# The end of a two-layer decoder trunk on one core: residual transposed into the accumulator, a root in PSUM, one eviction per bank, and a new order of the last parts

## The chip, the core and the metric

The kernel runs on one core of a Trainium2 chip. The metric is the device time in microseconds (us) of one execution; lower is better.

## What is computed

A stream of 2048 positions with 1024 features, all in float32, passes through two layers and a last normalisation. Cut to what matters here:

```python
h = rmsnorm(x, norm_a); b, c, xin, g = split(h @ w_in_a, 4)
x1 = x + (b * causal_conv3(c * xin) * silu(g)) @ w_out_a
k, v = split(rmsnorm(x1, norm_kv) @ w_kv, 2)
q, g = split(rmsnorm(x1, norm_b) @ w_in_b, 2)
o = stick_breaking_attention(q, k, v)        # 8 heads of 64, strictly causal
x2 = x1 + (o * silu(g)) @ w_out_b
out = rmsnorm(x2, norm_f)   # y * rsqrt(mean(y*y) + 1e-6) * norm_f
```

The change is mostly about the last two lines, for the last 128 positions. The root, `rsqrt`, is also used by every other normalisation.

## The kernel before

**Layout.** The input and the output are transposed: rows of 128 features lie on the partitions, positions along the free axis. The positions are cut into four chunks `c` of `CH` = 512. A float32 matrix product is made of three products of rounded halves (fp32r, a high and a low part), except for small ones in full float32 such as transposes, which the trace shows as one or two records each.

**Order.** Nearly all of the program is first recorded and then given an order by a planner; every instruction of it is emitted by one line (365), so rows of the profile are told apart by their tiles. Each piece of work belongs to a named part, and the table `PLAN` gives each part two numbers; an instruction's key is interpolated between them, and never lies before that of what it depends on (`places`). `order` then simulates the five engines with the estimated durations of `cost`: of what could start, it takes what could start first, and among equals that with the lower key. Numbers in `PLAN`, estimates in `cost` and dependencies all change which instruction stands before which in each engine's queue. An engine executes its queue in order. In `cost`, `o.turns` marks operations on DVE and POOL with more than one operand in SBUF and none in PSUM; the planner lets them take turns.

**Root.** `rstd` sums a tile of squares over the partitions by products with a column of ones, into a tile `pst_...`, and calls `rsqrt` (line 476). It makes `v` (mean plus epsilon), shifts it, makes a first guess `y` with one integer operation, and runs three steps of three operations on DVE, 12 operations in all:

```python
for _ in range(3):
    nc.vector.tensor_mul(t, y, y)
    nc.vector.scalar_tensor_tensor(out=t, in0=t, scalar=-0.5, in1=v, ...)
    nc.vector.scalar_tensor_tensor(out=y, in0=t, scalar=1.5, in1=y, ...)
```

`bcast` spreads the result over the partitions by four transposes on PE (`prb_...`); `pbs_...` is a copy of it in SBUF for POOL.

**The last layer.** In the names below, `ot` is an attention output, to which POOL adds `v_first` and which it multiplies by the gate `sga`; ACT rounds it to `og`. PE multiplies `og` by `wob` into a bank `pob`; DVE adds it to x1; squares are summed; and the tiles are multiplied by the broadcast root and stored, by POOL for chunks 0 and 1 and by DVE for chunk 2 (`out_kept`, `norm_kept`).

**The end.** `out_last(3)` treats the last chunk in two pieces. The first 384 positions go as above, with three of the eight tiles scaled by POOL (`x<-x,pbs`) and five by DVE (`x<-x,prb_x`). The last 128 positions are exchanged: positions lie on the partitions. While the first piece is computed, each x1 tile's last 128 columns are transposed by PE to `pt`, and ACT copies them to `turned`. Then 12 products with `og` as the stationary operand fill a bank `last` of 512 features, 24 in all for two halves. DVE adds `last` to `turned`; ACT squares it and sums along the row into `sums`; DVE adds the two sums to `total` and runs the root on one column (`v_last`, `t_last`, `yr_last`). DVE scales the identity by the root (`dg`), and PE multiplies blocks of `turned` by `dg`, which transposes back and scales at once, into a bank `back` per half. Each bank is evicted in four blocks of 128x128, ACT and DVE in turn, with the gain of each feature, into one tile `done`; SP's queue stores the first half and ACT's the second.

Behind it, outside of the planner's part, stands a branch with the whole attention done by another method, which runs only if a flag is set; it does not run here.

Of the kernel before, what the change touches and what calls it, by code (L numbers as in the profile page):

```python
# [16 lines left out]
P = 128  # L17
# [167 lines left out]
class Recorder:  # L185
# [30 lines left out]
    def cost(self, o, out, rest):  # L216
# [14 lines left out]
        if kind == PE:  # L231
            if o.name == "transpose":
# [141 lines left out]
def kernel(  # L374
# [967 lines left out]
    def out_last(c):  # L1342
# [14 lines left out]
        for ob in range(KD):  # L1357
# [3 lines left out]
            if ob % 4 == 0:  # L1361
                pt = psum.tile([P, CH], F32, name=f"pt_{c}_{ob}", tag="av", bufs=NAV)
            nc.tensor.transpose(pt[:, (ob % 4) * P:(ob % 4 + 1) * P], x[:, n:CH], ident)
            if ob % 4 == 3:
                nc.scalar.copy(turned[:, ob // 4, :], pt)
# [154 lines left out]
```

## Time and profile before

| | |
|---|---|
| time, median of 3 runs | 1344.25 us (1343.61 to 1344.61) |
| the profiled execution's own time | 1343.01 us |
| its span | 1341.2 us |
| mean granted PE clock | 0.993 |
| ACT busy | 601.9 us (45%) |
| POOL busy | 443.6 us (33%) |
| DMA | 364.99 MB, mean 272 GB/s |

The profile is of one execution. Its engines are PE (matrix products; PEld are PE's weight loads), DVE, ACT and POOL (element-wise work), and SP, which issues transfers; a "q" behind an engine's name stands for its queue of issues. In lists of groups each row gives engine, operation, output and inputs, partitions x elements of both, how often, then the busy time in us and the mean in ns of one, then the engine's idle time just before and what ended it. In lists by time each row starts with the start in us from the beginning of the span and the busy us. Where one row holds several instructions of a kind (x8), its time is that from the first's start to the last's end. A square bracket gives the idle time ahead of a row and who ended it.

### The profile page before, as it was taken

What the parts mean: (1) busy time and instruction counts of PE and PEld (TensorE: products, weight loads), DVE (VectorE), ACT (ScalarE), POOL (GpSimd) and SP (SyncE); (2) the same over time, 40 slices, a digit from 0 to 9 for tenths busy, and PEclk for the clock granted to TensorE, in tenths of its full rate; (3) what the DMA queues carried; (4) which work ended last, traced back from release to release, by engine and by line L of the source; (5) the groups of instructions that cost most, each with busy time, mean ns of one, the idle gap of its engine ahead of it and who ended that gap; (6) DMA issues with size and microseconds to landing.
All of it is one profiled execution on the core that took longest, in us unless ns stands there. A gap on an engine that the chain in (4) does not pass through costs nothing.

```text
span 1341.2 us, 19087 instructions
## 1 busy us (share of the span) xinstructions
PE 1305.6 (97%) x6222; PEld 1082.7 (81%) x6222; DVE 1026.6 (77%) x1626; ACT 601.9 (45%) x1062; POOL 443.6 (33%) x554
## 2 busy tenths in 40 slices
PE   8999999999999999999999999999999999999995
PEld 6888888888888888888788778788778888888884
DVE  7899866689964655656869579887998886898855
ACT  7344534444422332323334344544556554566652
POOL 5252110001000000010032454335357676458971
PEclk9999999999999999999999999999999999999997
DMA  9439879778898799987999876876787677999633
GB/s 327 169 131 325 283 270 326 280 280 292 309 353 287 257 353 334 318 293 244 357 324 325 302 261 209 274 252 230 240 305 233 194 230 244 341 335 310 223 136 128
DMA packets 213276, 364.99 MB, mean 272 GB/s; under 512 B 17028, under 2 KB 98992, under 8 KB 213168
## 3 DMA queue, kind: packets, MB, share of 16 engines
q1 hardware_dynamic: 211920, 362.61, 78.6%
q8 instruction: 51, 0.84, 0.2%
q10 hardware_dynamic: 1120, 1.05, 0.2%
q14 instruction: 57, 0.47, 0.1%
q0 software_dynamic: 128, 0.02, 0.0%
HBM read 217.35 MB, written 146.28 MB: 271 GB/s over the span
## 4 chain that ended last, share of the span: by engine, by line
PE 79%; DVE 12%; POOL 3%; issue 3%; ACT 2%; DMA 1%; SPq 0%; DVEq 0%; POOLq 0%; ACTq 0%
PE fa_C L365 11%; PE fa_B L365 10%; PE fa_o L365 6%; PE fa_kq L365 6%; PE fd_C L365 6%; PE fa_vg L365 5%; PE fd_B L365 5%; PE pob L365 3%; PE fd_vg L365 3%; PE fe_C L365 3%; PE fd_kq L365 3%; PE fd_o L365 3%; PE fe_B L365 3%; PE av L365 2%; PE fe_vg L365 1%
## 5 line engine op out<-in xcount | busy, mean ns | idle before, releaser
L365 POOL COPY halo<-p 128x2 f32<-128x2 f32 x32 | 16.3, 510 | 434.0 <-DVE p L365 434.0
L365 POOL TENSOR_TENSOR acc_x<-acc_x,sq_x 128x512 f32<-128x512 f32 (+1 forms) x53 | 75.8, 1434 | 121.8 <-ACT sq_x L365 121.0
L365 PE MATMUL pob<-og,wob 128*128 128x512 f32 (+1 forms) x384 | 103.6, 397 | 0.5 <-DVE x L365 0.5
L365 PE MATMUL fa_C<-op_t,whl_s_C 128*128 128x512 f32 x336 | 83.3, 389 | 0.0
L365 PE MATMUL fa_B<-op_t,whl_s_B 128*128 128x512 f32 x336 | 82.4, 390 | 0.2 <-ACT f_B L365 0.2
L365 DVE TENSOR_TENSOR_SCAN R<-R,ones 128x192 f32<-128x192 f32 x128 | 79.3, 657 | 2.0 <-POOL R L365 1.8
L365 PEld LDWEIGHTS fa_B<-op_t,whl_s_B 128*128 128x128 f32 x336 | 62.9, 188 | 13.6 <-ACT f_B L365 0.6
L365 PEld LDWEIGHTS fa_C<-op_t,whl_s_C 128*128 128x128 f32 x336 | 63.0, 188 | 13.1
L365 PEld LDWEIGHTS pob<-og,wob 128*128 128x128 f32 x384 | 65.2, 189 | 8.2 <-DVE x L365 0.9
L365 DVE SCALAR_TENSOR_TENSOR cv<-p,cols_of,cv 128x512 f32<-128x512 f32 x64 | 50.3, 787 | 11.0 <-ACT cv L365 10.8
L365 ACT ACTIVATE sq_x<-x 128x512 f32<-128x512 f32 (+1 forms) x56 | 34.4, 617 | 45.7 <-DVE x L365 34.1
L365 ACT CAST wth<-wt 128x512 fp32r<-128x512 f32 x64 | 36.4, 573 | 39.5 <-PE wt L365 19.7
L365 ACT ACTIVATE cv<-p,cols_of 128x512 f32<-128x512 f32 x32 | 23.2, 725 | 67.9 <-DVE p L365 67.9
L365 PE MATMUL wt<-ident,R 128*128 128x128 f32 x248 | 49.0, 274 | 1.5 <-DVE R L365 0.9
L365 POOL TENSOR_SCALAR_AFFINE_SELECT R<-R 128x256 f32<-128x256 f32 x64 | 36.0, 570 | 39.3 <-ACT R L365 39.1
L365 DVE TENSOR_TENSOR wtl<-wt,wth 128x512 fp32r<-128x512 f32 x64 | 42.0, 664 | 7.3 <-ACT wth L365 6.9
L365 PE MATMUL fa_C<-op_b,whl_a_C 128*128 128x512 f32 x168 | 43.1, 390 | 0.0
L365 PE MATMUL fa_B<-op_t,whl_a_B 128*128 128x512 f32 x168 | 43.0, 389 | 0.0
L365 PE MATMUL fe_B<-op_b,whl_a_B 128*128 128x512 f32 x168 | 42.9, 390 | 0.0
L365 PE MATMUL fd_C<-op_t,whl_s_C 128*128 128x512 f32 x168 | 42.3, 390 | 0.2 <-DVE op_t L365 0.2
L365 PE MATMUL fe_C<-op_b,whl_a_C 128*128 128x512 f32 x168 | 42.0, 389 | 0.0
L365 PE MATMUL fd_C<-op_b,whl_s_C 128*128 128x512 f32 x168 | 41.7, 390 | 0.0
(1039 smaller groups left out, 3846.2 us busy)
## 6 DMA issues: line engine op xcount, KB each, us to landing
sw_s_C<-whl_s_C SPq DMA_DIRECT2D x32, 512.0 KB, 3.9
sw_s_B<-whl_s_B SPq DMA_DIRECT2D x32, 512.0 KB, 4.2
q<-q_d SPq DMA_DIRECT2D x32, 512.0 KB, 5.7
sw_a_C<-whl_a_C SPq DMA_DIRECT2D x24, 512.0 KB, 3.3
sw_a_B<-whl_a_B SPq DMA_DIRECT2D x24, 512.0 KB, 3.3
whl_s_C<-sw_s_C SPq DMA_DIRECT2D x24, 512.0 KB, 5.4
whl_s_B<-sw_s_B SPq DMA_DIRECT2D x24, 512.0 KB, 5.3
whl_s_o<-sw_s_o SPq DMA_DIRECT2D x24, 512.0 KB, 5.3
```

The lines of the kernel that those rows point to most:

```text
L365: getattr(o.engine.engine, o.name)(*map(real, o.args), **{k: real(v) for k, v in o.kw.items()})
```

## The change

There are five edits.

- **Residual.** DVE copies the last 128 columns of each x1 tile to `x1_end`. PE transposes these eight blocks straight into the banks `last`, ahead of the products, which accumulate on top. The tile `pt` and the addition on DVE are gone. ACT squares the bank itself and copies it to `turned`, now one tile per half.
- **Root.** `newton` is split from `rsqrt`, for all roots: the first operation of a step is now `t = v * y` and the second multiplies by `-0.5 * y`. For the last root, `v` and `t` are columns of a PSUM tile `room`, so that operations with two tensor operands have one of them in PSUM. The first half's sum is scaled while the second half runs, and one operation scales the second and adds the two.
- **Eviction.** Each bank `back` is evicted by one DVE multiplication of 128x512, with the gains of four feature blocks broadcast along the free axis, into a buffer of its own.
- **Estimates.** `cost` takes transposing products as transposes, and the estimate of a one-column float32 product falls from 0.2 to 0.13.
- **`PLAN`.** The numbers of the last parts are others. A line of the table:

```diff
-    "n2": (1456.2, 1834.4), "o3": (2579.2, 2849.85), "n3": (1413.59, 1415.36), "le": (1301.17, 2112.05),
+    "n2": (2208.71, 2231.02), "o3": (2845.46, 3158.14), "n3": (1326.66, 1619.9), "le": (1768.92, 1896.9),
```

The code of the other edits:

```diff
-            if o.name == "transpose":
+            if o.name == "transpose" or o.kw.get("is_transpose"):
                 o.busy, o.late = 0.1085, 0.36
...
-                o.busy = (0.2 if n == 1 else 0.96 * n / 512) if full else max(0.109, 0.0135 + n / 2400)
+                o.busy = (0.13 if n == 1 else 0.96 * n / 512) if full else max(0.109, 0.0135 + n / 2400)
...
+        return newton(v, t, y)
+
+    def newton(v, t, y):
...
-        for _ in range(3):
-            nc.vector.tensor_mul(t, y, y)
-            nc.vector.scalar_tensor_tensor(out=t, in0=t, scalar=-0.5, in1=v, op0=ALU.mult, op1=ALU.mult)
+        for i in range(3):
+            nc.vector.tensor_mul(t, v, y)
+            nc.vector.scalar_tensor_tensor(out=t, in0=t, scalar=-0.5, in1=y, op0=ALU.mult, op1=ALU.mult)
             nc.vector.scalar_tensor_tensor(out=y, in0=t, scalar=1.5, in1=y, op0=ALU.add, op1=ALU.mult)
...
-            nc.tensor.transpose(pt[:, (ob % 4) * P:(ob % 4 + 1) * P], x[:, n:CH], ident)
-            if ob % 4 == 3:
-                nc.scalar.copy(turned[:, ob // 4, :], pt)
+            nc.vector.tensor_copy(x1_end[:, ob, :], x[:, n:CH])
...
+            for j in range(4):
+                nc.tensor.matmul(ps[:, j * P:(j + 1) * P], x1_end[:, 4 * half + j, :], ident, is_transpose=True, start=j == 0,
+                                 stop=False, skip_group_check=True)
...
-                    nc.tensor.matmul(ps, og_t[c][k][:, m, n:CH], wob[half][k][:, w, :], start=i == 0, stop=i == 11)
+                    nc.tensor.matmul(ps, og_t[c][k][:, m, n:CH], wob[half][k][:, w, :], start=False, stop=i == 11, skip_group_check=True)
...
-            row = turned[:, half, :]
-            nc.vector.tensor_add(row, row, ends[half])
-            nc.scalar.activation(sq, row, AF.Square, accum_out=sums[:, half:half + 1])
-        nc.vector.tensor_add(total[:, 0:1], sums[:, 0:1], sums[:, 1:2])
-        y = rsqrt(total, "last", n=1)
+            nc.scalar.activation(sq, ends[half], AF.Square, accum_out=sums[:, half:half + 1])
+            nc.scalar.copy(turned[half], ends[half])
+            if half == 0:
+                nc.vector.tensor_scalar(out=sums[:, 0:1], in0=sums[:, 0:1], scalar1=1.0 / D, scalar2=EPS, op0=ALU.mult, op1=ALU.add)
+        room = psum.tile([P, CH], F32, name="room", tag="av", bufs=NAV)
+        v, t = room[:, 0:1], room[:, 1:2]
+        nc.vector.tensor_scalar(out=v, in0=sums[:, 1:2], scalar1=1.0 / D, scalar2=sums[:, 0:1], op0=ALU.mult, op1=ALU.add)
+        newton(v, t, y_end)
...
-            for j in range(4):
-                if j % 2:
-                    nc.vector.tensor_scalar(out=done[:, half, blk], in0=ps[:, blk], scalar1=gains["f"][:, ob:ob + 1], ...)
-                else:
-                    nc.scalar.activation(done[:, half, blk], ps[:, blk], AF.Copy, scale=gains["f"][:, ob:ob + 1])
+            done = sb.tile([P, CH], F32, name=f"done_{half}", tag="vv", bufs=2)
+            nc.vector.tensor_mul(done.rearrange("p (j k) -> p j k", j=4), ps.rearrange("p (j k) -> p j k", j=4),
+                                 gains["f"][:, 4 * half:4 * half + 4].unsqueeze(2).to_broadcast([P, 4, P]))
```

The order of the instructions changes in many places. In the rows below a number after a name tells one buffer from another. DVE's queue at the very end, before the change, from the sum of the two halves on; the names with `last` are the root's columns, the five products scale tiles of the last chunk's first piece:

```order
L365 TENSOR_TENSOR total<-sums 128x1
L365 TENSOR_SCALAR v_last<-total 128x1
L365 TENSOR_SCALAR t_last<-v_last 128x1
L365 TENSOR_SCALAR yr_last<-t_last 128x1
L365 TENSOR_TENSOR x_3_0_12940<-x_3_0_12940,prb_x_13237 128x384
L365 TENSOR_TENSOR x_3_1_12965<-x_3_1_12965,prb_x_13237 128x384
L365 TENSOR_TENSOR x_3_2_13001<-x_3_2_13001,prb_x_13237 128x384 x2
L365 TENSOR_TENSOR x_3_3_13029<-x_3_3_13029,prb_x_13237 128x384
L365 TENSOR_TENSOR t_last<-yr_last 128x1
L365 SCALAR_TENSOR_TENSOR t_last<-t_last,v_last 128x1
L365 SCALAR_TENSOR_TENSOR yr_last<-t_last,yr_last 128x1
```

The same place after the change:

```order
L365 TENSOR_SCALAR room<-sums 128x1
L365 TENSOR_SCALAR room<-room 128x1
L365 TENSOR_TENSOR x_3_0_12936<-x_3_0_12936,prb_x_13240 128x384
L365 TENSOR_TENSOR x_3_1_12958<-x_3_1_12958,prb_x_13240 128x384
L365 TENSOR_TENSOR x_3_2_12993<-x_3_2_12993,prb_x_13240 128x384 x2
L365 TENSOR_TENSOR x_3_3_13026<-x_3_3_13026,prb_x_13240 128x384
L365 TENSOR_SCALAR yr_last<-room 128x1
L365 TENSOR_TENSOR room<-room,yr_last 128x1
L365 SCALAR_TENSOR_TENSOR room<-room,yr_last 128x1
L365 SCALAR_TENSOR_TENSOR yr_last<-room,yr_last 128x1
```

Four small operations ahead of the five products have become two; the guess `yr_last` has gone behind them, and no operation of the root has two operands in SBUF.

On POOL some 40 us before the end, with the attention outputs `ot_2` and `ot_3` of the last chunk, the scaling of chunk 1's eight tiles `x_1` and a copy `left` of the check for the flag, before the change:

```order
L365 TENSOR_TENSOR ot_2_12765<-ot_2_12765,v_first 128x512
L365 TENSOR_TENSOR ot_2_12765<-ot_2_12765,sga_2_12051 128x512
L365 TENSOR_TENSOR x_1_0_11936<-x_1_0_11936,pbs_12837 128x512
L365 COPY left<-R_7_1_12749 128x2
L365 TENSOR_TENSOR x_1_0_11936<-x_1_0_11936,pbs_12837 128x512
L365 TENSOR_TENSOR x_1_1_11960<-x_1_1_11960,pbs_12837 128x512 x2
L365 TENSOR_TENSOR x_1_2_12063<-x_1_2_12063,pbs_12837 128x512 x2
L365 TENSOR_TENSOR x_1_3_12442<-x_1_3_12442,pbs_12837 128x512 x2
L365 TENSOR_TENSOR acc_x_12577<-acc_x_12577,sq_x_12833 128x512
L365 TENSOR_TENSOR ot_3_11429<-ot_3_11429,v_first 128x512
```

The same place after the change:

```order
L365 TENSOR_TENSOR ot_2_12312<-ot_2_12312,v_first 128x512
L365 TENSOR_TENSOR x_1_0_11883<-x_1_0_11883,pbs_12834 128x512 x2
L365 TENSOR_TENSOR x_1_1_12013<-x_1_1_12013,pbs_12834 128x512 x2
L365 TENSOR_TENSOR x_1_2_12064<-x_1_2_12064,pbs_12834 128x512 x2
L365 TENSOR_TENSOR x_1_3_12141<-x_1_3_12141,pbs_12834 128x512 x2
L365 TENSOR_TENSOR ot_2_12312<-ot_2_12312,sga_2_11950 128x512
L365 TENSOR_TENSOR ot_3_12757<-ot_3_12757,v_first 128x512
L365 TENSOR_TENSOR ot_3_12757<-ot_3_12757,sga_3_12232 128x512
```

The gate of `ot_2` stood ahead of the eight products of `x_1` and now stands behind them; the sum and the gate of `ot_3` follow without squares between.

On DVE at the beginning of the program, with the first chunk's eight normalised tiles `h_0` to `h_7` and the first root (`v_h`, `t_h`, `yr_h`), - is before and + after:

```order
 L365 SCALAR_TENSOR_TENSOR h_0_557<-xh_0_489,g_a,h_0_557 128x512
+L365 TENSOR_SCALAR v_h_679<-pst_h_663 128x4
+L365 TENSOR_SCALAR t_h_683<-v_h_679 128x4
+L365 TENSOR_SCALAR yr_h_685<-t_h_683 128x4
+L365 TENSOR_TENSOR t_h_683<-v_h_679,yr_h_685 128x4
 L365 SCALAR_TENSOR_TENSOR h_1_572<-xh_1_496,g_a,h_1_572 128x512
-L365 TENSOR_SCALAR v_h_681<-pst_h_663 128x4
-L365 TENSOR_SCALAR t_h_685<-v_h_681 128x4
-L365 TENSOR_SCALAR yr_h_688<-t_h_685 128x4
-L365 TENSOR_TENSOR t_h_685<-yr_h_688 128x4
+L365 SCALAR_TENSOR_TENSOR t_h_683<-t_h_683,yr_h_685 128x4
 L365 SCALAR_TENSOR_TENSOR h_2_605<-xh_2_515,g_a,h_2_605 128x512
```

The first four operations of the root have moved ahead of the product `h_1`; `h_1` has moved behind them.

More of the change, by code (lines that the diff above doesn't have):

```diff
@@ L1354, in out_last @@
         late = []
-        turned = sb.tile([P, 2, CH], F32, name="turned", tag="act", bufs=NA)
-        pt = None
+        turned = [sb.tile([P, CH], F32, name=f"turned_{i}", tag=("wth", "wtl")[i], bufs=NWTS) for i in range(2)]
+        x1_end = sb.tile([P, KD, P], F32, name="x1_end", tag="q2", bufs=2)
         for ob in range(KD):
@@ L1360, in out_last @@
             tag, bufs = (("lin", NLIN), ("z", NZ))[ob % 2]
-            if ob % 4 == 0:
-                pt = psum.tile([P, CH], F32, name=f"pt_{c}_{ob}", tag="av", bufs=NAV)
-            nc.tensor.transpose(pt[:, (ob % 4) * P:(ob % 4 + 1) * P], x[:, n:CH], ident)
-            if ob % 4 == 3:
-                nc.scalar.copy(turned[:, ob // 4, :], pt)
+            nc.vector.tensor_copy(x1_end[:, ob, :], x[:, n:CH])
             ps = psum.tile([P, CH], F32, name=f"pob_{c}_{ob}", tag=tag, bufs=bufs)
@@ L1406, in out_last @@
         for half in range(2):
-            row = turned[:, half, :]
-            nc.vector.tensor_add(row, row, ends[half])
-            sq = sb.tile([P, CH], F32, name=f"sq_last_{half}", tag="q2", bufs=2)
-            nc.scalar.activation(sq, row, AF.Square, accum_out=sums[:, half:half + 1])
-        total = sb.tile([P, 4], F32, name="total", tag="sv")
-        nc.vector.tensor_add(total[:, 0:1], sums[:, 0:1], sums[:, 1:2])
-        y = rsqrt(total, "last", n=1)
+            sq = sb.tile([P, CH], F32, name=f"sq_last_{half}", tag="kt", bufs=2)
+            nc.scalar.activation(sq, ends[half], AF.Square, accum_out=sums[:, half:half + 1])
[4 more added lines that the diff above has]
+        v, t = room[:, 0:1], room[:, 1:2]
+        y_end = sb.tile([P, 4], F32, name="yr_last", tag="sy")[:, 0:1]
+        nc.vector.tensor_scalar(out=v, in0=sums[:, 1:2], scalar1=1.0 / D, scalar2=sums[:, 0:1], op0=ALU.mult, op1=ALU.add)
+        newton(v, t, y_end)
         dg = sb.tile([P, P], F32, name="dg", tag="q2", bufs=2)
-        nc.vector.tensor_scalar(out=dg, in0=ident, scalar1=y, scalar2=None, op0=ALU.mult)
-        done = sb.tile([P, 2, CH], F32, name="done", tag="act", bufs=NA)
+        nc.vector.tensor_scalar(out=dg, in0=ident, scalar1=y_end, scalar2=None, op0=ALU.mult)
         for half in range(2):
@@ L1419, in out_last @@
             for j in range(4):
-                nc.tensor.matmul(ps[:, j * P:(j + 1) * P], turned[:, half, j * P:(j + 1) * P], dg, start=True, stop=True)
-            for j in range(4):
-                ob = 4 * half + j
-                blk = slice(j * P, (j + 1) * P)
-                if j % 2:
-                    nc.vector.tensor_scalar(out=done[:, half, blk], in0=ps[:, blk], scalar1=gains["f"][:, ob:ob + 1], scalar2=None, op0=ALU.mult)
-                else:
-                    nc.scalar.activation(done[:, half, blk], ps[:, blk], AF.Copy, scale=gains["f"][:, ob:ob + 1])
+                nc.tensor.matmul(ps[:, j * P:(j + 1) * P], turned[half][:, j * P:(j + 1) * P], dg, start=True, stop=True)
+            done = sb.tile([P, CH], F32, name=f"done_{half}", tag="vv", bufs=2)
+            nc.vector.tensor_mul(done.rearrange("p (j k) -> p j k", j=4), ps.rearrange("p (j k) -> p j k", j=4),
+                                 gains["f"][:, 4 * half:4 * half + 4].unsqueeze(2).to_broadcast([P, 4, P]))
             (nc.scalar if half else nc.sync).dma_start(
                 out=outT[4 * half * P:4 * (half + 1) * P, S - CH * c - P:S - CH * c].rearrange("(k p) n -> p k n", p=P),
-                in_=done[:, half, :].rearrange("p (k n) -> p k n", k=4))
+                in_=done.rearrange("p (j k) -> p j k", j=4))
     def part(name, f, *args):
```

26 rows, old and new, of the table PLAN are left out of this document.

## The prediction, made before the changed kernel was run

> **What bounds the kernel now.** I read the page first, then who waits on TensorE, then the chain of work that ended last, and at its end the instructions in order of time.
>
> ```profile
> span 1341.2 us, 19087 instructions
> PE 1305.6 (97%) x6222; PEld 1082.7 (81%) x6222; DVE 1026.6 (77%) x1626; ACT 601.9 (45%) x1062; POOL 443.6 (33%) x554
> PE back L365 <- DVE dg L365: 5.2, 1, 5.2
> ```
>
> PE is busy for 1305.6 of 1341.2 us, so for 35.6 us it isn't. The longest wait of its list (columns: total, times, longest), 5.2 us, lies at the end. Whatever PE executes is the same number of instructions before and after the change, so only gaps can be won or lost. The last gap runs from the last product `last` to the end of the span, and the chain shows it piece by piece (columns: start us, us, engine, tile):
>
> ```profile
> 1320.15 1.50 PE last L365 x6
> 1321.75 0.69 DVE turned L365
> ...
> 1323.99 2.41 DVE x L365 x5
> 1326.40 0.45 DVE t_last L365
> 1326.87 0.93 DVE t_last L365
> ...
> 1328.02 0.17 DVE t_last L365
> ...
> 1329.18 0.30 DVE dg L365
> 1329.52 1.66 PE back L365 x6
> ...
> 1331.63 2.09 PE back L365 x8
> 1333.74 0.38 ACT done L365
> 1334.16 0.81 PE back L365 x2
> ...
> 1335.78 0.35 DVE done L365
> ```
>
> I call the end of `last`, 1320.15 + 1.50 = 1321.65, T0. From T0 to the scaled identity `dg` (ready at 1329.48) pass 7.83 us, mostly on DVE; from there to the last eviction (1336.13) 6.65 us, in which PE and the evictions of one bank take turns. These instructions stand behind and beside it:
>
> ```profile
> 1312.93 4.87 DVE L365 TENSOR_TENSOR x<-x,prb_x 128x512 f32<-128x512 f32 x8 [1.01 <-PE prb_x L365]
> 1322.47 0.63 ACT L365 ACTIVATE sq_last<-turned 128x512 f32<-128x512 f32 x1 [2.38 <-DVE turned L365]
> 1323.01 0.19 ACT L365 ACTIVATION_READ_ACCUMULATOR sq_last<-turned 128x1 f32 x1
> 1323.44 0.51 PE L365 MATMUL prb_x<-ident,yr_x 128*128 128x128 f32 x3 [1.80 <-DVE total L365]
> 1324.87 2.90 POOL L365 TENSOR_TENSOR x<-x,pbs 128x384 f32<-128x384 f32 x3 [14.39 <-ACT pbs L365]
> 1336.17 0.39 ACTq L365 DMA_DIRECT2D out_dram<-done  x1
> ```
>
> The last store is issued at 1336.17 (T0 + 14.52), and 5.03 us later the span is over. That remainder has the same store of the same size in both kernels: I leave it as it is.
>
> **The change part by part.** *From T0 to `dg`.* Gone are the addition of the residual (0.69 us and its hand-over), `total`, and half of the wait for `prb_x`. ACT now squares the bank itself. It can start where DVE's addition started, T0 + 0.10, and takes 0.54 us to its accumulator read (1322.47 to 1323.01) and 0.19 us for that: T0 + 0.83. Two operations on the column follow (v and its shift), 0.19 us apart as the chain's 1328.02 pieces are with their 0.02 of issue: T0 + 1.24. Then come the five products of x, 2.41 us, as before: T0 + 3.67. The chain of x's own root, 12 small operations, stood in DVE's queue behind the residual's addition; now it stands behind `sums`. Ahead of `sums` in turn stand eight products of x_2 (4.87 us), which wait for a `prb_x` that PE now issues 24 products `last` and six transposes of 0.11 before T0, 6.6 us (four such took 0.44, in a row further below); the first half's squares are read at T0 - 3.0 + 0.73. So x's root starts some 1.6 us before T0, and 12 x 0.195 us ends it at T0 + 0.7. `prb_x` (0.51 us) is then there at T0 + 1.2, as the shift of v ends: its 1.8 us of waiting is covered by ACT's squares.
>
> What is left before `dg` are one integer operation and nine of the root. Two of these took 0.45 and 0.93 us where their like take 0.17: they ended at 1326.85 and 1327.80, when the second and the third of POOL's three products ended (2.90 / 3 = 0.97 us each from 1324.87). All three products have both operands in SBUF, like the operations that waited; the five products of x, which read one operand from PSUM, ran undisturbed in the same time. With v and t in PSUM every operation of the root has at most one operand in SBUF, so I take no such wait. 10 x 0.195 = 1.95 us, then 0.32 for `dg`: T0 + 5.94 instead of T0 + 7.83. **1.9 us gained.**
>
> The unknown is what a DVE operation costs that writes to PSUM; the trace has none. Rows for reading from there:
>
> ```profile
> L365 DVE TENSOR_SCALAR v_x<-pst_x 128x3 f32<-128x3 f32 x1 | 0.2, 160 | 1.2 <-PE pst_x L365 1.2
> L365 DVE TENSOR_SCALAR v_last<-total 128x1 f32<-128x1 f32 x1 | 0.2, 154 | 0.0
> L365 DVE TENSOR_SCALAR done<-back,cols_of 128x128 f32<-128x128 f32 x4 | 1.4, 352 | 5.3 <-PE back L365 4.4 <-ACT done L365 0.9
> ```
>
> Reading a column from PSUM took 160 ns, from SBUF 154. Below I set 0 for the write (no row shows SBUF writes to be slower than PSUM's); above, what `done` of 128x128, read from PSUM, takes more than `dg` of the same size between SBUF tiles, 352 ns against 0.30 us: 0.05 us for each operand in PSUM, 19 of them in the root with v and its shift, 0.95 us. I take 0, as the rows of one column are the nearest in size, and keep both ends. The Trainium skill speaks against this edit: "Perfetto Trace Analysis", section "Optimizing Scalar/DVE Operations", gives some 60 ns of access overhead for DVE on SBUF and some 125 ns on PSUM. By it 19 operands would lose an estimated 1.2 us; the 6 ns between the first two rows above don't show it for reads.
>
> *From `dg` to the last store.* Before, each bank was evicted in blocks by two engines, and the products for the second bank waited for evictions. Eight blocks are 16 records of PE: 8 records took 2.09 us and 2 took 0.81, so 0.213 us for each further record, and 16 take 0.81 + 14 x 0.213 = 3.79 us. Each bank has now its own buffer and one DVE operation of 128x512; the nearest row is the residual's addition, of the same size with one PSUM operand and a full second one: 0.69 us (the second operand is now a repeated gain column, which no row has). Four blocks of 0.35 us bound it above at 1.4, 0.7 us dearer; I take the row of the same size. The first eviction lies beside the second bank's products. 0.04 + 3.79 + 0.02 + 0.69 = 4.54 us in place of 6.65: **2.1 us gained.** The two stores move with the evictions, from T0 + 14.52 to T0 + 10.52. ACT's copies of the two banks (the square of such a tile takes 0.63 us) end by T0 + 1.6, beside DVE's chain, which lasts 4 us longer; without that cover they would cost 0.6 us.
>
> *The residual.* Eight copies of 128x128 come on DVE and eight transposes leave one place of PE for another; the two copies `turned<-pt` leave ACT and two come back at the end. PE's count is unchanged. The eight copies, 8 x at most 0.35 us (the row of `done`, which has that shape), lie beside PE's products 10 us before T0: nothing, unless the adds queued behind them are late.
>
> *The beginning.* The planner's price for a one-column product fell, and the root's operations read v and y in another order; both move instructions from the first us on. On DVE the product h_1 now comes behind the first four steps of the first root:
>
> ```profile
> 26.63 6.52 POOL L365 TENSOR_TENSOR acc_h<-acc_h,sq_h 128x512 f32<-128x512 f32 x4 [1.54 <-ACT sq_h L365]
> 27.32 0.16 DVE L365 TENSOR_SCALAR v_h<-pst_h 128x4 f32<-128x4 f32 x1 [0.36 <-PE pst_h L365]
> 29.43 0.74 DVE L365 SCALAR_TENSOR_TENSOR h<-xh,g_a,h 128x512 fp32r<-128x512 f32 x1
> 36.34 0.16 DVE L365 SCALAR_TENSOR_TENSOR yr_h<-t_h,yr_h 128x4 f32<-128x4 f32 x1
> 36.65 0.62 PE L365 MATMUL prb_h<-ident,yr_h 128*128 128x128 f32 x4 [0.87 <-DVE yr_h L365]
> ```
>
> DVE waited 0.36 us for `pst_h` with h_1 done already; from then on the root and six further h (h_2 to h_7) shared it with POOL's four products. Now seven h stand between that wait and the last `yr_h`, so it ends one h later (0.74 us), while `prb_h` has moved behind one more product of PE, which is of the size of the 0.25 us of a `last`. PE's wait of 0.87 us grows by 0.74 - 0.25 = **0.5 us lost**; between 0 and 1.6, for POOL could take one more turn of 6.52 / 4.
>
> *Between.* For the stretch from there to T0 the columns are its ends, its length, then busy time of PE, of its weight loads, of DVE, ACT and POOL, the granted clock, and the DMA's share and rate:
>
> ```profile
> 37.27:1321.65 1284.38, 1269.91 (x6077) 1054.41 (x6075) 991.27 (x1557) 575.68 (x1015) 420.56 (x527) 1.00 0.80 273
> ```
>
> PE is idle for 1284.38 - 1269.91 = 14.5 us of it. In the middle the order is untouched, in the last 600 us most rows have moved a little. The place with the greatest move is POOL's: the eight products of x_1 now precede the gate of `ot_2`, which was ahead of them.
>
> ```profile
> 1278.81 2.38 PE pob L365 x10
> 1281.19 0.44 PE prb_x L365 x4
> ...
> 1294.36 4.22 PE pob L365 x24
> ```
>
> ```profile
> 1282.03 0.59 ACT L365 COPY pbs<-prb_x 128x512 f32<-128x512 f32 x1
> 1283.26 1.31 POOL L365 TENSOR_TENSOR x<-x,pbs 128x512 f32<-128x512 f32 x1
> 1284.63 9.30 POOL L365 TENSOR_TENSOR x<-x,pbs 128x512 f32<-128x512 f32 x7
> 1295.82 1.04 POOL L365 TENSOR_TENSOR ot<-ot,v_first 128x512 f32<-128x512 f32 x1 [0.64 <-DVE ot L365]
> 1298.07 1.29 POOL L365 TENSOR_TENSOR ot<-ot,sga 128x512 f32<-128x512 f32 x1
> ```
>
> From the end of `prb_x` (1281.63) `pbs` took 0.99 us, eight products 1.31 + 9.30 = 10.6, the gate 1.3 and ACT's `og`, a tile like `pbs`, 0.6: og_2 at 13.5 us. PE has by the order 45 products of 512 columns (2.38 / 10 each), 19 of 384 (4.22 / 24) and 12 transposes (0.44 / 4) before it needs it: 10.7 + 3.3 + 1.3 = 15.3. og_3 follows at 13.5 + 1.04 + 1.29 = 15.8, needed 16 products of 384 later, at 18.1. Both are in time by 1.8 us or more; I count 0 for the whole stretch, with 1 us less and 2.5 us more as bounds (of its 14.5 us of idle time, a fifteenth and a sixth).
>
> **Sum.** -1.9 - 2.1 + 0.5 = -3.5 us on the profiled execution's 1343.01 (its span and 1.8 us around it): 1339.5. That execution lies 1.24 us below the median of the three runs, 1344.25, against which the result will stand: 1340.75.
>
> **Rivals.** *(a) The new forms are dear*, the writes to PSUM and the eviction with a repeated operand. For it: no row shows either. They give back up to 0.95 + 0.7 us: 1342.4.
>
> *(b) PE's clock stays up for part of `back`.* The granted clock is the third number from the end:
>
> ```profile
> 1324.00:1326.00 2.00, 0.28 (x3) 0.03 (x1) 2.00 (x5) 0.48 (x1) 1.13 (x2) 0.88 0.30 114
> 1334.00:1336.00 2.00, 0.80 (x2) 0.50 (x2) 0.57 (x2) 0.48 (x2) 0.00 (x0) 0.50 0.48 143
> ```
>
> If it fell from full to half once in the first stretch (mean 0.88), it did so about 1325.5, 3.9 us after T0, though PE worked at 1323.44. `back` ran at half clock, beginning 7.87 us after T0; now it begins 5.98 after. If the fall comes up to 3.8 us later in another execution, `back` runs at full clock, half of 3.79 us: 1.9 us less, 1338.9. Against it: 5 us of idle time remain. The Trainium skill ("TensorE: Matmul & The Clock Gate", section "Part 1: The HAM clock gate") says that the gate judges free-running windows of some 3.4 us, which would make this a matter of where the window falls; the one fall in this trace cannot show that.
>
> *(c) New waits on PE in the stretch between.* For it: nearly every row of the last 600 us has moved, and the order follows from estimated durations, while the 14.5 us of idle time above show where such estimates miss. Between 1 and 2.5 us back; with 1.75, 1342.5. It is also the case in which the new order is worse than the old and eats half of what the end gains.
>
> *(d) Slower: POOL's queue.* Ahead of the eight products stand the addition and the gate of `ot_1`, two sums of squares and `ot_2`'s addition, 1.04 + 1.29 + 2 x 1.3 + 1.04 = 6 us, which wait on DVE. If they run only after `pbs` is there, og_2 comes 6 us late, and from 1.8 us on each is PE's. With POOL and DVE taking turns, another 1.31 for each of the two gates: 6 + 2.6 - 1.8 = 6.8 us lost on 1340.75, 1347.5. Against it: before the change POOL began these products 0.64 us after `pbs` (1282.62 to 1283.26), with one gate more already behind it.
>
> **How the numbers follow.** Forecast 0.50; (a) 0.12; (b) 0.15; (c) 0.17; (d) 0.06. A difference of 0.2% (2.7 us) is about what a measurement of this kernel can tell from no change, so faster means below 1341.55: four fifths of the forecast's cases, (b), and a quarter of (a), 0.58. Slower by that needs 1346.95: most of (d), 0.05. The rest is 0.37. The range reaches down to (b) with the lower bound of the stretch between, 1337.9, and up to (c) with half of the other upper bounds (0.95, 0.7 and, at the beginning, 1.6 - 0.5), 2.5 + 1.4 above the forecast, 1344.65; outside are (d) and the corner where all meet.
>
> **What would show it.** In the new profile: `room` operations at 0.16 to 0.17 us each, none above 0.3; eight blocks of `back` without a wait between; two `done` of 0.69 us; the last store 10.5 us after the last `last`; `prb_h` waiting 1.4 us near 37 us; no wait of PE on `og`. The forecast is wrong if `room` steps last 0.25 us, if PE's idle time between 37 us and T0 is much other than 14.5 us, or if `back` still stops between banks.

## The result: 0.33% slower

The changed kernel took 1348.78 us (median of 8 runs, 1346.36 to 1350.99) against 1344.34 us of the kernel before beside it (8 runs, 1342.98 to 1346.80). The ratio is 1.0033, with a 95% interval of 1.0022 to 1.0044. The forecast was 1340.75 us, faster, with a range up to 1344.65.

The page of the changed kernel's profile (own time 1348.82 us) has the same number of PE records:

```profile
span 1347.0 us, 19081 instructions
PE 1308.1 (97%) x6222; PEld 1082.2 (80%) x6222; DVE 1020.0 (76%) x1630; ACT 597.3 (44%) x1058; POOL 440.5 (33%) x554
```

The end is read first, since it was forecast in most detail. The chain of waits of the changed kernel, from the last products `last` on (start us, us, engine, tile):

```profile
1326.31 4.72 PE last L365 x22
1331.05 0.70 ACT sq_last L365 x2
1331.77 0.23 DVE room L365
1332.03 0.17 DVE room L365
1332.19 2.31 DVE x L365 x5
...
1334.61 0.18 DVE room L365
...
1336.38 0.30 DVE dg L365
1336.82 3.67 PE back L365 x16
1340.51 0.69 DVE done L365
```

T0, the end of the last `last`, is 1326.31 + 4.72 = 1331.03. `dg` is ready 5.65 us later (7.83 before, 5.94 forecast), the last eviction ends 4.52 us after that (6.65 before, 4.54 forecast): 4.31 us gained. But T0 itself is 9.38 us later than before (1331.03 against 1321.65). And the last store takes longer from issue to landing; the transfers of the end, of before and of the changed kernel (engine of the queue, KB each, us to landing):

```profile
out_dram<-done ACTq DMA_DIRECT2D x1, 256.0 KB, 3.1
```

```profile
out_dram<-done ACTq DMA_DIRECT2D x1, 256.0 KB, 3.9
```

9.38 - 4.31 = 5.07 us, and 0.7 to 0.8 for the store, make the span's growth of 5.8 us. The time was not lost at the end but ahead of it. To find where, the same event is sought in both traces. A product `fa_o` that waits about 1.1 us for `x` stands in both; in order of time on PE, before and after:

```profile
644.80 0.97 PE L365 MATMUL fa_o<-op_t_('o', 0)_0_5765,whl_s_o 128*128 128x512 f32 x3 [1.09 <-DVE x L365]
```

```profile
651.51 0.96 PE L365 MATMUL fa_o<-op_t_('o', 0)_0_5765,whl_s_o 128*128 128x512 f32 x3 [1.09 <-DVE x L365]
```

Of the 9.38 us, 6.71 are there before the middle of the program is reached. The prediction held that "only gaps can be won or lost". The row of the stretch from 37 us to T0, which it shows for the kernel before, is now:

```profile
37.27:1331.03 1293.76, 1274.14 (x6079) 1055.24 (x6077) 987.67 (x1570) 572.38 (x1014) 418.18 (x527) 1.00 0.79 271
```

PE is idle for 19.6 us instead of 14.5, and it is also busy for 4.2 us more with the same products: 5.2 and 4.2 make the 9.4. The windows of 300 to 400 us (columns as in the prediction), before and after:

```profile
300.00:400.00 100.00, 99.76 (x439) 81.90 (x438) 87.42 (x135) 42.52 (x73) 10.36 (x16) 1.00 0.90 317
```

```profile
300.00:400.00 100.00, 95.67 (x413) 76.28 (x412) 86.30 (x135) 41.99 (x71) 12.25 (x16) 1.00 0.91 320
```

PE executes 26 records fewer in the same 100 us and idles for 4.3 us where it idled for 0.2. At the 0.227 us a record of the kernel before, 26 records are an estimated 5.9 us: the longer idle time and 1.8 us besides. In the rows below the first product behind a wait takes 0.50 us and each further one 0.23, so a restart costs about a quarter of a microsecond beside the wait. Of the 6.71 us, the other 0.8 lie ahead of 300 us. The waits of this stretch, in order of time on PE, in the changed kernel (in the brackets the wait and what ended it):

```profile
325.76 0.50 PE L365 MATMUL fe_B<-op_b,whl_a_B 128*128 128x512 f32 x1 [1.02 <-DVE whl_a_B L365]
...
340.13 0.73 PE L365 MATMUL fd_B<-op_b,whl_s_B 128*128 128x512 f32 x2 [0.48 <-ACT whl_s_B L365]
...
353.40 0.96 PE L365 MATMUL fa_C<-op_t,whl_s_C 128*128 128x512 f32 x3 [1.07 <-DVE op_t L365]
354.66 0.74 PE L365 MATMUL fa_C<-op_t,whl_s_C 128*128 128x512 f32 x2 [0.30 <-DVE op_t L365]
...
355.86 0.73 PE L365 MATMUL fe_C<-op_b,whl_a_C 128*128 128x512 f32 x2 [0.23 <-DVE op_b L365]
357.18 0.50 PE L365 MATMUL fe_C<-op_b,whl_a_C 128*128 128x512 f32 x1 [0.58 <-ACT op_b L365]
358.33 0.73 PE L365 MATMUL fe_C<-op_b,whl_a_C 128*128 128x512 f32 x2 [0.66 <-DMA xb_('o', 0)_0_3518<-y_d]
```

In the kernel before PE has no wait over 0.2 us between 320 and 390 us. What PE waits for are weights of B (`whl_a_B`, `whl_s_B`) and operands `op_t`, `op_b`, made by DVE and ACT, and once a transfer. DVE's last preparation of B's weights for this stage, before; and after, the last two and the first operands made ahead of them:

```profile
314.40 0.68 DVE L365 TENSOR_TENSOR whl_s_B<-fr_a_B,whl_s_B 128x512 fp32r<-128x512 f32 x1
```

```profile
315.85 1.90 DVE L365 TENSOR_TENSOR op_b<-xb,op_b 128x512 fp32r<-128x512 f32 x3
...
338.70 0.68 DVE L365 TENSOR_TENSOR fr_a_B<-fr_a_B,fr_a_B 128x512 f32<-128x512 f32 x1
340.56 0.68 DVE L365 TENSOR_TENSOR whl_s_B<-fr_a_B,whl_s_B 128x512 fp32r<-128x512 f32 x1
```

What DVE had done by 315 us is done 26 us later. In between it made operands (`op_b`, `op_t`) for chunk 2, from 315.85 on, which before the change came behind the weights. Nothing released DVE late here: it worked without a pause, in the order of its queue.

The last 2.67 of the 9.38 us arise behind 645 us. Part of them belongs to this one execution. Two windows just behind the next root, in the changed kernel and at the same work before:

```profile
736.00:740.00 4.00, 4.00 (x12) 3.15 (x11) 4.00 (x20) 2.21 (x4) 0.00 (x0) 0.57 0.58 206
```

```profile
729.30:733.30 4.00, 4.00 (x19) 3.29 (x18) 4.00 (x20) 2.20 (x4) 0.00 (x0) 1.00 0.88 299
```

The granted clock was 0.57 there instead of 1.00, and PE executed 12 records instead of 19, an estimated 1.6 us. The profile of the next section's first run, with the same order of PE here, has a clock of 1.00 in the same window. The kernel before has such a fall of its own, 0.57 from 786 to 790 us. So single profiles can't be compared to a microsecond behind 645 us: in four of the kernels below PE has the same queue from first to last, and their T0 lies 676.5 to 680.3 us behind `fa_o`.

### The profile page after: what moved, and what is told of

It reads as the page before. It is cut to its first block, busy times and chain, and to the rows that moved or that the text cites. A ratio compares the mean times of both kernels' runs of the same rounds, so it can differ in the third digit from the quotient of the medians.

```text
span 1347.0 us, 19081 instructions
## 1 busy us (share of the span) xinstructions
PE 1308.1 (97%) x6222; PEld 1082.2 (80%) x6222; DVE 1020.0 (76%) x1630; ACT 597.3 (44%) x1058; POOL 440.5 (33%) x554
## 4 chain that ended last, share of the span: by engine, by line
PE 79%; DVE 11%; issue 3%; DMA 2%; ACT 2%; POOL 1%; SPq 0%; DVEq 0%; POOLq 0%; ACTq 0%
PE fa_C L365 10%; PE fa_B L365 10%; PE fa_o L365 6%; PE fa_kq L365 6%; PE pob L365 5%; PE fd_C L365 5%; PE fd_B L365 5%; PE fa_vg L365 4%; PE fd_o L365 3%; PE fd_kq L365 3%; PE fe_C L365 3%; PE fe_B L365 2%; PE av L365 2%; PE fd_vg L365 2%; PE wt L365 2%
## 5 line engine op out<-in xcount | busy, mean ns | idle before, releaser
L365 POOL COPY halo<-p 128x2 f32<-128x2 f32 x32 | 13.5, 421 | 415.5 <-DVE p L365 415.4
L365 PE MATMUL pob<-og,wob 128*128 128x512 f32 (+1 forms) x384 | 99.4, 392 | 0.0
L365 PEld LDWEIGHTS fa_C<-op_t,whl_s_C 128*128 128x128 f32 x336 | 62.7, 188 | 16.4 <-DVE op_t L365 3.1
L365 PE MATMUL z<-kt,q 128*128 128x192 f32 x256 | 41.8, 278 | 0.3 <-DMA kt<-k_d 0.3
```

The lines of the kernel that those rows point to most:

```text
L365: getattr(o.engine.engine, o.name)(*map(real, o.args), **{k: real(v) for k, v in o.kw.items()})
```

## Theories

**A**: the planner's lower estimate of a one-column product, 0.2 to 0.13, gives the first 380 us another order, and this is the loss. **B**: the new numbers of the last parts did it. **C**: the new order of factors in all roots did it. **D**: the end's edits cost time ahead of the end. In the traces, the estimate alone changes PE's queue in places up to 374 us and again from 730 us on, up to the end; the roots' factors alone don't change it at all.

## Experiments: which edit

**The estimate alone**, in the kernel before:

```diff
-                o.busy = (0.2 if n == 1 else 0.96 * n / 512) if full else ...
+                o.busy = (0.13 if n == 1 else 0.96 * n / 512) if full else ...
```

> The kernel before, with nothing changed but the planner's estimate of a one-column product, 0.2 to 0.13. Theory A (the lower estimate reorders the first 380 us, and that is where the time went): PE reaches the product fa_o that waits 1.09 us for x at 651.5 us instead of 644.8, DVE prepares the last pieces of the weights B at 324 to 341 us, PE waits several times between 340 and 359 us, the end from the last product `last` to the last eviction stays at 14.5 us, and the time is 1344.3 + 6.7 = 1351 us, with up to 3 us more from the stretch of 670 to 955 us, which moves too. Theory B (the new numbers of the last parts did it, and the early shift belongs to one profile): 1344.3 us within 1 us, fa_o at 645 us.

1357.01 us; ratio 1.0093 (1.0079 to 1.0108). PE's rows in order of time:

```profile
353.36 0.96 PE L365 MATMUL fa_C<-op_t,whl_s_C 128*128 128x512 f32 x3 [1.11 <-DVE op_t L365]
```

```profile
651.47 0.98 PE L365 MATMUL fa_o<-op_t_('o', 0)_0_5765,whl_s_o 128*128 128x512 f32 x3 [1.08 <-DVE x L365]
```

`fa_o` stands where theory A put it, with a wait at 353 us like that of the changed kernel. The time rose by 11.7 us, more than by A's 6.7 with up to 3 more. The end, expected to stay at 14.5 us from the last `last` to the last eviction, took 15.5 (1331.48 to 1346.99): PE's order differs there too. B's 1344.3 us fails; that the new numbers have no part in the loss is shown by the fourth run.

**The roots' factors alone**, in the kernel before:

```diff
-            nc.vector.tensor_mul(t, y, y)
-            nc.vector.scalar_tensor_tensor(out=t, in0=t, scalar=-0.5, in1=v, ...)
+            nc.vector.tensor_mul(t, v, y)
+            nc.vector.scalar_tensor_tensor(out=t, in0=t, scalar=-0.5, in1=y, ...)
```

> The kernel before, with the new order of factors (t = v * y first) in all roots and nothing else. PE's order does not change by it, DVE's around the roots does. Theory C (the roots' new order delays what PE waits for early): part of the 6.7 us is here, 1347 us or more, fa_o with its 1.09 us of waiting later than 646 us. Theories A and B: 1344.3 us within 0.7 us.

1344.97 us, ratio 1.0002 (0.9993 to 1.0011). C fails.

**The end's edits alone**: the changed kernel with the table and the estimate of before. Of the table's lines one is shown.

```diff
...
-    "n2": (2208.71, 2231.02), "o3": (2845.46, 3158.14), "n3": (1326.66, 1619.9), "le": (1768.92, 1896.9),
+    "n2": (1456.2, 1834.4), "o3": (2579.2, 2849.85), "n3": (1413.59, 1415.36), "le": (1301.17, 2112.05),
...
-                o.busy = (0.13 if n == 1 else 0.96 * n / 512) if full else ...
+                o.busy = (0.2 if n == 1 else 0.96 * n / 512) if full else ...
```

> The changed kernel's residual, roots and evictions, with the numbers of all parts and the estimate 0.2 of before; its order on PE is that of before up to the last parts. Theory A: the end as in the changed kernel, 10.2 us from the last product `last` to the last eviction instead of 14.5, nothing lost ahead of it: 1344.3 - 4.3 + 0.7 = 1340.7 us, within 1 us. Theory D (the end's edits cost time ahead of the end, by eight copies on DVE, or by what moved with them): 1343 us or more, with PE's idle time between 37 us and the last `last` over 16 us.

1341.85 us, ratio 0.9972 (0.9957 to 0.9987). From the last `last` to the last eviction it has 9.98 us (1324.49 to 1334.47). As the cause of the loss D fails, but the result lies between the theories: the time is 1.1 us over A's value and under D's 1343, while PE idles for 16.4 us between 37 us and T0, which is D's sign, and T0 is 2.84 us later than before. Part of that is again a fall of the clock (0.57 from 729 to 733 us); that the end's edits cost up to about 1 us ahead of the end is not excluded.

**The lower estimate for the last parts only**: the changed kernel, with its new table. `LAST` is the set of the parts of the attention and behind it (names with `a`, `g`, `o`, `n`, and `fl`, `le`).

```diff
-                o.busy = (0.13 if n == 1 else 0.96 * n / 512) if full else ...
+                o.busy = ((0.13 if o.part in LAST else 0.2) if n == 1 else 0.96 * n / 512) if full else ...
```

> The changed kernel, with the estimate 0.13 only in the last parts and 0.2 as before in all others: on PE the order of before up to about 955 us, from about 1050 us on that of the changed kernel. Theory A: fa_o at 644.8 us, end as in the changed kernel. If the new order of the last parts gains nothing, 1340.7 us; if it is the reason for the other 2.7 us that PE was late at the last `last`, 1343.4 us. Theory B: 1348.8 us stays, within 1.5 us.

1340.48 us, ratio 0.9971 (0.9962 to 0.9980). This is the lowest median of all kernels here: all edits of the change are in it, and only the estimate of the earlier parts is as before. T0 is 1321.54, within 0.2 us of the kernel before, and PE reaches `fa_o` at 645 us:

```profile
645.06 0.97 PE L365 MATMUL fa_o<-op_t_('o', 0)_0_5765,whl_s_o 128*128 128x512 f32 x3 [1.09 <-DVE x L365]
```

So the whole loss goes with that estimate. Against the run with the end's edits and the old table the ratios to before are the same within their intervals. So the new numbers of the last parts gain nothing that can be measured here, where the earlier order is kept.

## Experiments: why the estimate

16 of the one-column products, those of the first four roots, lie ahead of 280 us. Lowering their estimate by 0.07 shortens the planner's account of them by 1.1 us in all. Two readings are possible: that the lower number is wrong, or that any other number than 0.2 would have done the same. In the trace six records of `pst_x`, three products, take 0.56 us on the chain of the kernel with the estimate split: 0.19 us for each.

```profile
1316.31 0.56 PE pst_x L365 x6
```

**0.19 instead of 0.2**, everywhere, in the kernel before; in the next run **0.3**:

```diff
-                o.busy = (0.2 if n == 1 else 0.96 * n / 512) if full else ...
+                o.busy = (0.19 if n == 1 else 0.96 * n / 512) if full else ...
```

> The kernel before, with the estimate 0.19 instead of 0.2 everywhere. Theory A1 (a product taken as shorter makes the planner start roots too early, by as much as it is too short): a seventh of the 11.7 us that 0.13 cost, 1347 us. Theory A2 (the table of numbers fits the order that came with 0.2, and any other estimate changes that order for one that was not searched): as much as with 0.13, 1350 to 1360 us.

> The kernel before, with the estimate 0.3 instead of 0.2 everywhere. Theory A1: the other direction, so no loss of this kind, 1345 us or a little less. Theory A2: again another order that was not searched, 1350 us or more.

1356.48 us (ratio 1.0087, 1.0070 to 1.0104) and 1356.18 us (1.0079, 1.0056 to 1.0103). Both cost 11 us: the number that fits the trace, one far above it, and 0.13 alike. Theory A1 fails and what A2 expected came: it is the pair of the table and 0.2 that makes the good order. That the table was searched with 0.2 is inferred and not shown, and why all three other values push the same preparations back was not taken apart. In all three the last weights of B come late, at 327 and 341 us in the run with 0.19 (DVE in order of time):

```profile
327.26 0.68 DVE L365 TENSOR_TENSOR whl_s_B<-fr_a_B,whl_s_B 128x512 fp32r<-128x512 f32 x1
...
341.55 0.67 DVE L365 TENSOR_TENSOR whl_s_B<-fr_a_B,whl_s_B 128x512 fp32r<-128x512 f32 x1
```

**The first four roots only**, which lie in parts whose names begin with `m` or `s`:

```diff
-                o.busy = (0.2 if n == 1 else 0.96 * n / 512) if full else ...
+                o.busy = ((0.13 if o.part[0] in "msx" else 0.2) if n == 1 else 0.96 * n / 512) if full else ...
```

> The kernel before, with the estimate 0.13 for the 16 one-column products of the first four roots alone (all of them in the first 280 us) and 0.2 for the others. PE's order differs from that of before only ahead of about 385 us. If the loss of the early stretch stays in the time (theory A): fa_o at 651.5 us instead of 644.8, and 1345.3 + 6.7 = 1352 us, within 1.5; the rest of the 11.7 us of the run with the estimate changed everywhere then comes from the roots behind 670 us. If later waits absorb it: fa_o late, but under 1349 us.

1353.44 us, ratio 1.0064 (1.0046 to 1.0081): 8.2 us, 1.4 more than expected and within the interval (6.2 to 10.9). `fa_o` stands at 653.2 us, but 1.6 us of that are there at 118 us already, in a row that stands at 116.2 to 116.3 us in the other profiles with this order. No later wait absorbs the loss. The median is 3.6 us below that with the estimate changed everywhere; the two intervals just overlap, and the stretch behind 730 us, where the two kernels differ, was not taken apart. So whether the later roots cost anything is not shown.

**The late weights undone.** The same kernel, but the preparation of the last weights of B gets a lower key and so goes first again where DVE has a choice:

```diff
-            o.key = t0 + (t1 - t0) * k / count[o.part]
+            o.key = t0 + (t1 - t0) * k / count[o.part]; o.key -= 40 * (o.part == "m07" and 30 < o.key < 50)
```

> As the run with 0.13 for the first four roots alone, but with the keys of the part that prepares the last pieces of the weights C and B lowered by 40 for these preparations. By the order, DVE then has the preparation of the last pieces of B again ahead of the operands of chunk 2. Theory P (their late preparation is what PE waits for, and what then crowds DVE at 340 to 360 us): fa_o at 645 to 646.5 us, 1345.3 + 1 = 1346 us. Theory Q (the whole reordered stretch is worse, at many places): 1351 us or more, as without the lowered keys (1353.4).

1345.90 us, ratio 1.0003 (0.9994 to 1.0012): the loss is gone. DVE in order of time, then PE:

```profile
323.28 0.68 DVE L365 TENSOR_TENSOR whl_s_B<-fr_a_B,whl_s_B 128x512 fp32r<-128x512 f32 x1
```

```profile
645.34 0.98 PE L365 MATMUL fa_o<-op_t_('o', 0)_0_5765,whl_s_o 128*128 128x512 f32 x3 [1.30 <-DVE x L365]
```

The last piece is prepared at 323 us instead of 342, and between 320 and 390 us PE has no wait over 0.2 us. The lower keys go to 40 instructions: 16 on DVE, 9 on ACT, 4 on POOL and 11 transfers. Most prepare these weights; a few belong to the convolution of the same part, so the run shows it for this part and not for the weights by themselves. That PE pays for the late weights, and for what they push together behind them, is read from its waits for them. The lower estimate is still there, and PE's order of the first 280 us with it.

## Experiments: the parts of the end

All three undo one edit of the end in the kernel with the estimate split (1340.48 us; from the last `last` to `dg` 5.66 us, from `dg` to the last eviction 4.62).

**v and t of the last root in SBUF again.** The order of all engines stays.

```diff
-        room = psum.tile([P, CH], F32, name="room", tag="av", bufs=NAV)
-        v, t = room[:, 0:1], room[:, 1:2]
+        v = sb.tile([P, 4], F32, name="v_last", tag="sv")[:, 0:1]
+        t = sb.tile([P, 4], F32, name="t_last", tag="st")[:, 0:1]
```

> The changed kernel with the estimate 0.13 in the last parts alone (1340.5 us), and the last root's v and t in SBUF again; the order of all engines stays. Theory W (two SBUF operands make DVE wait for POOL's product): the root's first operations behind DVE's five products of x take 0.3 to 0.9 us where they took 0.18, the stretch from the last `last` to dg is 6.4 to 6.7 us instead of 5.66. Theory P (PSUM costs more than such waits): the stretch is 5.66 us or less, with no operation of the root over 0.2 us.

The chain of waits:

```profile
1325.34 1.01 DVE t_last L365
...
1326.37 0.17 DVE t_last L365
...
1327.92 0.30 DVE dg L365
```

One operation, with both operands in SBUF, takes 1.01 us instead of 0.18 and ends at 1326.35, as the last of POOL's three products does (1323.42 to 1326.32). In the kernel with `room` these products run from 1323.18 to 1326.08, and no operation of the root beside them takes over 0.2 us. `dg` is now ready 6.44 us after the last `last` (1321.78 to 1328.22): 0.78 us more. Theory W holds. The time, 1341.92 us (ratio 0.9977, 0.9967 to 0.9988), rises by less than can be told apart, also since the last store landed after 2.9 us in this profile and 3.7 in that of the kernel with `room`. What a write to PSUM costs, by the groups of DVE at the end, in this run and in the changed kernel (times, busy us, mean ns):

```profile
L365 DVE SCALAR_TENSOR_TENSOR t_last<-t_last,yr_last 128x1 f32<-128x1 f32 x3 | 0.5, 159 | 0.1
```

```profile
L365 DVE SCALAR_TENSOR_TENSOR room<-room,yr_last 128x1 f32<-128x1 f32 x3 | 0.5, 166 | 0.1
```

7 ns for an operation that reads and writes there.

**Four blocks by two engines again**, into one tile `done`, in place of one eviction per bank.

```diff
-            done = sb.tile([P, CH], F32, name=f"done_{half}", tag="vv", bufs=2)
-            nc.vector.tensor_mul(done.rearrange("p (j k) -> p j k", j=4), ps.rearrange("p (j k) -> p j k", j=4), ...)
+            if half == 0:
+                done = sb.tile([P, 2, CH], F32, name="done", tag="act", bufs=NA)
+            for j in range(4):
+                if j % 2:
+                    nc.vector.tensor_scalar(out=done[:, half, blk], in0=ps[:, blk], scalar1=gains["f"][:, ob:ob + 1], ...)
+                else:
+                    nc.scalar.activation(done[:, half, blk], ps[:, blk], AF.Copy, scale=gains["f"][:, ob:ob + 1])
```

> The changed kernel with the estimate 0.13 in the last parts alone (1340.5 us), and the banks `back` evicted as before, in four blocks by ACT and DVE in turn into one tile. From dg to the last eviction 6.65 us as before instead of 4.62. If nothing is given back behind it, the time is 2.0 us longer; if the last store lands 0.7 us sooner because the two stores are issued 2.5 instead of 1.7 us apart, 1.3 us longer.

1341.97 us (ratio 0.9981, 0.9972 to 0.9990). The last eviction ends 12.37 us after the last `last` (1322.90 to 1335.27) instead of 10.28: 2.1 us, as expected; the last store lands in 3.1 us. The median is 1.5 us higher, with intervals that overlap: the trace shows this gain, the time alone does not.

**The residual added by DVE again.**

```diff
-            nc.vector.tensor_copy(x1_end[:, ob, :], x[:, n:CH])
...
+            nc.tensor.transpose(pt[:, (ob % 4) * P:(ob % 4 + 1) * P], x[:, n:CH], ident)
+            if ob % 4 == 3:
+                nc.scalar.copy(turned[:, ob // 4, :], pt)
...
-                nc.tensor.matmul(ps[:, j * P:(j + 1) * P], x1_end[:, 4 * half + j, :], ident, is_transpose=True, start=j == 0, ...)
...
-            nc.scalar.activation(sq, ends[half], AF.Square, accum_out=sums[:, half:half + 1])
-            nc.scalar.copy(turned[half], ends[half])
+            row = turned[:, half, :]
+            nc.vector.tensor_add(row, row, ends[half])
+            nc.scalar.activation(sq, row, AF.Square, accum_out=sums[:, half:half + 1])
```

> The changed kernel with the estimate 0.13 in the last parts alone (1340.5 us), and the residual as before: transposed to a bank of its own while the first piece is computed, copied by ACT, added by DVE. From the last `last` to the first square 0.75 us more (the addition and its hand-over); x's root, which stands behind it on DVE, later by as much. The stretch from the last `last` to dg is 6.4 to 7.2 us instead of 5.66, the time 0.7 to 1.5 us longer. If ACT's wait for the addition was hidden: 5.7 us.

1342.88 us (ratio 0.9982, 0.9973 to 0.9991). The chain of waits:

```profile
1323.57 0.69 DVE turned L365
...
1329.79 0.96 DVE dg L365
```

`dg` is ready 7.29 us after the last `last` (1323.46 to 1330.75) instead of 5.66: 1.6 us, just above what was expected. Part of it is `dg` itself, 0.96 us instead of 0.30: in this order it comes to lie beside POOL's products (1327.75 to 1330.65). The median is 2.4 us higher, and the intervals overlap here too.

**The last store.** In the profiles so far the second `done` landed 3.7 to 3.9 us after its issue where ACT's queue had issued a store of x 4.2 to 5.7 us ahead, from issue to issue, and 2.9 to 3.1 us where 6.2 us or more lay between. With ACT's stores of x moved to SP's queue:

```diff
-            (nc.scalar if k % 2 else nc.sync).dma_start(out=outT[k * P:(k + 1) * P, ...], in_=x2[k][:, 0:n])
+            nc.sync.dma_start(out=outT[k * P:(k + 1) * P, ...], in_=x2[k][:, 0:n])
```

> The changed kernel with the estimate 0.13 in the last parts alone (1340.5 us), and the four stores of the last chunk's first piece that ACT's queue issues moved to SP's; nothing else moves. So far the last store took 3.7 to 3.9 us from its issue to landing where ACT's queue had issued other stores 4.2 to 5.1 us earlier, and 2.9 to 3.1 where 5.8 to 8.4 us lay between. Theory S (the earlier stores of its own queue hold it up): 2.9 to 3.1 us now, the time 0.7 us less, 1339.8 us. Theory T (the transfers themselves do, whatever the queue, or the nearness of the other `done`, 1.7 us before): 3.7 us or more, 1340.5 us.

```profile
out_dram<-done ACTq DMA_DIRECT2D x1, 256.0 KB, 3.6
```

3.6 us, and 1341.95 us (ratio 0.9970, 0.9959 to 0.9981): theory S fails. The nearness of the other `done` alone does not explain it either, since with v and t in SBUF the same 1.7 us lay between the two and it landed in 2.9. What is left of theory T, the other stores whatever their queue, fits all profiles here: where the last store of x, of either queue, was issued 4.2 to 5.6 us ahead, it took 3.6 to 3.9 us, and where 6.2 to 8.6 us ahead, 2.9 to 3.1. This was sorted afterwards and not tested, so what decides stays open.

## Why the prediction was wrong, point by point

- **The step that failed** is "I count 0 for the whole stretch", with 1 us less and 2.5 us more as bounds, and ahead of it "In the middle the order is untouched". It treated the stretch from 37 us to T0 as one and looked for the danger at its end, on POOL. That instructions move "from the first us on" was said, but only the first root was priced. The stretch cost 9.4 us, and with the estimate of the earlier parts as before it costs nothing. 6.7 of them are there by 645 us, of these 5.9 between 300 and 400, and there the runs show the cause: the estimate moves the preparation of the last weights on DVE behind operands for chunk 2. The other 2.7 us, an estimated 1.6 of them a fall of the clock in that execution, stay open.
- **A premise that failed** is "only gaps can be won or lost". PE's busy time in the stretch grew by 4.2 us with the same products, nearly as much as its gaps did with 5.2: in part by the restarts behind waits, in part by the fall of the clock. The sign that the prediction named, an idle time much other than 14.5 us, came with 19.6.
- **The beginning** was priced at 0.5 us for `prb_h`. Its wait was 1.0 us instead of 0.9, so that term was too dear. That 0.8 us are lost ahead of 300 us all the same does not bear it out: nearly all of them arise between 100 and 125 us, at products that it had not priced. The main harm of the same edit came 300 us later.
- **From T0 to `dg`**: 2.2 us gained, 1.9 forecast. Its two parts are shown each by a run: with v and t in SBUF, 0.78 us come back, since an operation with two operands in SBUF waits for POOL's product; with the residual added by DVE, 1.6 us come back, 0.66 of them at `dg` beside POOL. The Trainium skill ("SBUF — State Buffer", section "SBUF: two separate sides") has a rule for it: a DVE operation with two SBUF inputs and a GpSimd operation that reads SBUF exclude each other for a whole instruction. The 1.01 us of the operation beside a product of 0.97 us agree with it.
- **From `dg` to the last eviction**: 2.1 us gained, as forecast; the run with four blocks by two engines gives the same 2.1 back.
- **What was left as it is**, the stretch behind the last store's issue, grew by 0.7 us. It had not been counted.
- **Rivals.** (a), dear new forms: no, 7 ns for an operation of the root with PSUM and 0.69 us for the eviction. (b), the clock: the rows below are of the changed kernel. It fell to half about 1336.9, 5.9 us after T0 and not 3.9, and `back` ran at half clock again. What the prediction calls the one fall in its trace was not the only one, as the window of 786 to 790 us named above shows. (c), new waits in the stretch between, named the right kind of event and the wrong place, with a bound a quarter of what came. (d), POOL's queue, did not occur: PE has no wait for `og`.

```profile
1335.00:1337.00 2.00, 0.18 (x1) 0.21 (x2) 1.42 (x8) 0.00 (x0) 0.57 (x1) 0.98 1.06 363
1337.00:1339.00 2.00, 2.00 (x11) 2.00 (x10) 0.18 (x1) 0.00 (x0) 0.00 (x0) 0.50 0.44 158
```

Without the lower estimate in the earlier parts the forecast's sum would have been met: 1340.48 us against 1340.75. That agrees with the terms that it did work out for the end; that it agrees to 0.3 us is luck, since the run that differs only in the queue of four stores has 1341.95, and it is not evidence for the account of the rest.

## What to carry to other kernels

Where a planner makes the order out of estimates and a table that was fitted to them, an estimate is part of the table. Changing it, even to the value that the trace shows, can give another and worse order, everywhere the estimate occurs and not only where one meant it. So compare the order of every stretch, not only of the edited one, and look for preparation work that has slid behind work whose result nobody waits for yet; such a slide is paid when the result is due, here 10 to 45 us after DVE had turned to the other work. A wait of PE also costs more than its idle time, here 1.8 us on 4.1. And if an estimate has to change, confine it to the parts whose numbers are searched anew.

## What the runs showed of the hardware

- A write to PSUM by a one-column DVE operation is nearly free: 166 ns where the same operation between SBUF columns took 159.
- The last store of 256 KB took either 2.9 to 3.1 or 3.6 to 3.9 us to land, in kernels whose end differs little. Neither its own queue's earlier stores nor the distance to the other `done` decides that; the long times are those with a store of x, of either queue, issued at most 5.6 us ahead.
- PE's clock fell 3.9 us after the last product `last` in the kernel before and 5.9 us after it in the changed one, though in both only the short products of `prb_x` lie between it and `back`.
- In the middle of the program the granted clock falls in some executions and not in others: 0.57 over 4 us in the profile of the changed kernel, 1.00 in that of the estimate alone, at the same work.
